# Two layers of chosen tokens get the row gather of a third, more weight pieces, and some operations tied to program order

## The chip, the cores and the metric

The kernel is one program on one core of one Trainium2 chip. Its time is the device time of one execution in microseconds. The core has engines that each take their instructions in order: PE (TensorE, matrix products), DVE (VectorE), ACT (ScalarE), POOL (GpSimd) and SP (SyncE, which here only issues transfers); ACT and POOL issue transfers too.

## The reference, cut to what matters

Two blocks run one after the other on 512 tokens of width 1024, everything in float32. The first mixes tokens and then sends each token to 2 of 64 experts. The second has two layers; each mixes tokens and then lets each of 16 experts choose 64 tokens:

```python
def expert_choice_ffn(h, router, w_gate, w_up, w_down):
    cap = EC_CAPACITY_FACTOR * n // N_EXPERTS_2          # 64
    aff = softmax(einsum('bnd,de->bne', h, router))
    gate, idx = lax.top_k(aff.transpose(0, 2, 1), cap)
    xg = h[bidx, idx]
    hid = silu(einsum('becd,edf->becf', xg, w_gate)) * einsum('becd,edf->becf', xg, w_up)
    y = einsum('becf,efd->becd', hid, w_down) * gate[..., None]
    return zeros_like(h).at[bidx, idx].add(y)
```

The input h of that function is a normalized and modulated x: `modulate(rms_norm(x, g), shift, scale)`, with shift and scale out of products of a conditioning vector with wide weights (w_mod in the first block, ada_w in the second). Each expert has 3 weight matrices of 2 MB.

## The kernel before, in words

Tokens lie as h, four tiles of 128 tokens by 1024. There are six stages in order: the first mixing stage, the 64-expert layer, the second mixing stage, the first expert-choice layer, the third mixing stage, the second expert-choice layer.

**Order.** Each stage is a set of generators that a planner (`weave`) steps by planned times; that gives the program order. The instructions then go to a scheduler that may put an instruction ahead of earlier ones on its engine when it takes its inputs to be there sooner. `keep_in_program_order(ins)` ties an instruction behind the one that precedes it on its engine in the program. Weights come by SP's transfers in the order of queues, into places that come free in turn (`pump`, L295).

**Products of a mixing stage** (`gemms`, L364) take fp32r parts: each weight piece is split into a high part by ACT (L386) and a low part, the rest, by DVE (L387), and each product is three. `split2` (L448, L449) does the same for single tiles. `rsqrt` (L168 to L173) is an inverse square root by some 14 small operations on DVE; its result scales a diagonal dg (L219) by which TensorE transposes and normalizes a tile. `mod_sum` (L2201 to L2207) multiplies rows of modulation weights by the conditioning vector and adds them up, on DVE and, where it shares, on POOL. In the first stage yd, a DRAM buffer of 4096 KB that the 64-expert layer scatters to, is filled by a POOL transfer (L686).

**The 64-expert layer** (`experts1`) works on pairs of experts. xd, a DRAM copy of the normalized rows, is written by the stage before it (`tail`, L2328). For each pair: P (L1262) is 1 where a token is in a place of an expert; four products (pid) give each place's row number; POOL gathers 128 rows xg of xd (L1250); eight TensorE transposes (pxt) turn them; ACT and DVE copy them with scale and shift into xT, 128 columns at a time (L1313, L1316). Pair 0 doesn't wait for xd: Pr = P times the normalizing factor (L1269), and 32 fp32 products of h with Pr give the same pxt.

**The expert-choice layers** (`ec`, L2591, with `experts`, L1089) find the 64th largest affinity by repeated top-8 on DVE, and from it the place of each token. x, the normalized rows, is split into fp32r parts xh and xl (`split_x`, `split_rest`), 32 KB a partition together. Four experts at a time, P (L1112) is built and 64 products pdis, 128 by 256, of xh and xl with P give xT, in two halves, by TensorE alone. Each pair then has 16 steps of gate and up products (pab), 4 transposes (phT), the down products (py), and products that add the results back to their tokens (pcm). Weights come as pieces of 512 KB in 24 places: 6, 9 and 9 in the first layer, 9 and 15 in the second.

```python
for part, x in enumerate((self.xh, self.xl)):
    self.mm(o, self.fcol(x[:, i], k), rhs, start=(i == 0 and part == 0), ...)
```

Of the kernel before, what the change touches and what calls it, by code (L numbers as in the profile page):

```python
# [137 lines left out]
class Kern:  # L138
# [23 lines left out]
    def rsqrt(self, pool, v, shape, tag):  # L162

        nc = self.nc
        ib = pool.tile(shape, I32, tag=tag + "i", name=tag + "i")
        y = pool.tile(shape, F32, tag=tag + "y", name=tag + "y")
        t = pool.tile(shape, F32, tag=tag + "t", name=tag + "t")
        nc.vector.tensor_scalar(ib, v.bitcast(I32), 1, None, op0=ALU.logical_shift_right)  # L168
        nc.vector.tensor_scalar(y.bitcast(I32), ib, -1.0, float(0x5F3759DF), op0=ALU.mult, op1=ALU.add)
        for _ in range(3):  # L170
            nc.vector.tensor_tensor(t, y, y, op=ALU.mult)
            nc.vector.scalar_tensor_tensor(t, t, -0.5, v, op0=ALU.mult, op1=ALU.mult)
            nc.vector.scalar_tensor_tensor(y, t, 1.5, y, op0=ALU.add, op1=ALU.mult)  # L173
        return y
# [189 lines left out]
    def gemms(self, items, pool, nb=2):  # L364
# [6 lines left out]
        def parts():  # L371
            for it in items:
                w, big = it["w"], None
                for c in it.get("order") or range(len(w.ev)):
# [11 lines left out]
                    nc.scalar.copy(hi, raw)  # L386
                    nc.vector.tensor_tensor(lo, raw, hi.bitcast(F32), op=ALU.subtract)  # L387
# [58 lines left out]
    def split2(self, hi, lo, x):  # L446

        self.nc.scalar.copy(hi, x)  # L448
        self.nc.vector.tensor_tensor(lo, x, hi.bitcast(F32), op=ALU.subtract)  # L449
# [34 lines left out]
    def run(self):  # L484
# [7 lines left out]
        self.nB, self.nX, self.nE = 14, 12, 24  # L492
# [65 lines left out]
    def mix1(self):  # L558
# [70 lines left out]
        def consts():  # L629
# [3 lines left out]
            yield 15000  # L633
            self.split2(wgh, wgl, wg)
# [17 lines left out]
        def start():  # L652
# [20 lines left out]
            for v, s in ((1, sx), (0, sl)):  # L673
# [6 lines left out]
                else:  # L680
# [5 lines left out]
            nc.gpsimd.dma_start(self.yd.rearrange("(p r) d -> p r d", p=128),  # L686
                                am.rearrange("p a b c t -> p (a b c t)").unsqueeze(1).to_broadcast([128, 2 * T // 128, D]))
# [300 lines left out]
        items = [item(wkc, sx, True, 2, k_in(sx), [sx.evx]), item(wvc, sx, False, 2, v_in(sx)),  # L988
# [25 lines left out]

    def split_x(self, pool):

        nc = self.nc
        for i in range(NT):
            if i < 3:
                t = pool.tile([128, D], F32, tag="xn", name="xn", bufs=2)  # L1020
                x = nc.scalar.activation(t, self.h[:, i, :], AF.Copy, scale=self.r[:, i:i + 1])
                if i == 0:
                    self.tc.keep_in_program_order(x)
                nc.scalar.copy(self.xh[:, i, :], t)
                for q in range(2):
                    c = slice(q * 512, (q + 1) * 512)
                    nc.gpsimd.tensor_tensor(self.xl[:, i, c], t[:, c], self.xh[:, i, c].bitcast(F32), op=ALU.subtract)
            else:
                nc.scalar.activation(self.xh[:, i, :], self.h[:, i, :], AF.Copy, scale=self.r[:, i:i + 1])

    def split_rest(self):
        for q in range(2):
            c = slice(q * 512, (q + 1) * 512)
            for i in range(3, NT):
                x = self.nc.vector.scalar_tensor_tensor(self.xl[:, i, c], self.h[:, i, c], self.r[:, i:i + 1], self.xh[:, i, c].bitcast(F32),
                                                        op0=ALU.mult, op1=ALU.subtract)
                self.tc.keep_in_program_order(x)

    def x_tiles(self, st, ne):
        xp = st.enter_context(self.pool("x", 1))  # L1040
        self.xh = xp.tile([128, NT, D], F32R, name="xh")
        self.xl = xp.tile([128, NT, D], F32R, name="xl")
        self.G = self.gates(ne)
        return xp
# [44 lines left out]
    def experts(self, ne, ws, pool, work, last=None):  # L1089


        nc = self.nc
        io = self.iota[:, 0:CAP]
        ng = ne // 4
        rX, rA, rY, rP = Res(2), Res(4), Res(3), Res(4)
        self.ny = 3
        evx, evy = [Ev() for _ in range(ng)], {(pr, c): Ev() for pr in range(ne // 2) for c in range(2)}
        xTs, PTs, gs, yos = {}, {}, {}, {}
        self.evf, evg = ([Ev() for _ in range(ne // 2)] for _ in range(2))

        evk = [Ev() for _ in range(KD // 2)]

        def dispatch(g):
            if g:
                yield evx[g - 1]
            yield rX
            yield rP
            yield rP
            es = slice(4 * g, 4 * g + 4)
            P = pool.tile([128, NT, 4, CAP], F32R, tag="P", name="P")  # L1110
            for i in range(NT):
                nc.vector.tensor_tensor(P[:, i], self.slot[:, i, es].unsqueeze(2).to_broadcast([128, 4, CAP]),  # L1112
                                        io.unsqueeze(1).to_broadcast([128, 4, CAP]), op=ALU.is_equal)
            if not g and ne == NE2:
                self.split_rest()
            xT = pool.tile([128, KD, 256], F32, tag="xT", name="xT", bufs=2)
            xTs[g] = xT
            yield 1500
            def transposed():
                for q in range(2):  # L1120
                    p = self.ps(name="ppt")
                    pp = lambda i: P[:, i, 2 * q:2 * q + 2, :].rearrange("p e s -> p (e s)").bitcast(F32)
                    for i in range(NT):
                        self.tr(p[:, i * 128:(i + 1) * 128], pp(i))
                    t = work.tile([128, T], F32R, tag="PT", name="PT", bufs=4)
                    nc.scalar.copy(t, p)
                    p = self.ps(name="pgt")
                    for i in range(NT):
                        self.mm(p[:, 0:2], pp(i), self.G[:, i, 4 * g + 2 * q:4 * g + 2 * q + 2], start=(i == 0), stop=(i == NT - 1))
                    gt = work.tile([128, 1], F32, tag="gt", name="gt", bufs=4)  # L1130
                    for j in range(2):
                        nc.vector.tensor_copy(gt[64 * j:64 * j + 64, :], p[64 * j:64 * j + 64, j:j + 1])
                    PTs[2 * g + q], gs[2 * g + q] = t, gt
                    self.fire(evg[2 * g + q], 800)
                    yield 0

            if g:
                yield from transposed()
            for k2 in range(KD // 2):
                p = self.ps(name="pdis")  # L1140
                for kk in range(2):
                    k = 2 * k2 + kk
                    o = p[:, kk * 256:(kk + 1) * 256]
                    for i in range(NT):
                        rhs = P[:, i].rearrange("p e s -> p (e s)")
                        for part, x in enumerate((self.xh, self.xl)):
# [13 lines left out]
        def ffn(pr):  # L1160
# [6 lines left out]
            for ws2 in up:  # L1167
                yield rA
                p = self.psum.tile([128, 512], F32, tag="a", name="pab", bufs=4)
                for k in range(KD):  # L1170
# [3 lines left out]
                    if k == 3:  # L1174
                        yield 0
# [1624 lines left out]
```

## Time and profile before

| | |
|---|---|
| runs of the kernel, us | 2719.69, 2713.5, 2715.77; median 2715.77 |
| profiled execution, us | 2713.79 |
| its span from the first to the last instruction, us | 2712.0 |
| mean granted TensorE clock (of full speed) | 0.957 |
| PE busy | 2353.7 us, 87% |
| DVE busy | 1121.4 us, 41% |
| ACT busy | 655.8 us, 24% |
| POOL busy | 261.2 us, 10% |
| moved by DMA | 772.76 MB, 285 GB/s on the mean |

Busy time is summed over stages with different limits, so it says little of the end; the profile's views by stretch, by wait and by time do. A wait is put down to what came last for it. In a timeline, the bracket is the idle time of the engine before the instruction and what ended it. The stages can be found by their time: the first mixing stage ends near 385 us, the 64-expert layer near 1503, the first expert-choice layer runs from about 1899 to 2182, the second from about 2418.

### The profile page before, as it was taken

How to read it: one execution, taken by the hardware profiler on the slowest of the kernel's cores; microseconds unless marked ns; L12 is line 12 of the kernel's file. 1: busy time of each engine (PE TensorE's matmuls, PEld its weight loads, DVE VectorE, ACT ScalarE, POOL GpSimd, SP SyncE). 2: the span in 40 equal slices, each digit the busy share in tenths (PEclk: the TensorE clock that was granted, in tenths of full speed). 3: DMA queues.
4: the chain of work that ended last, by engine and by line, in shares of the span. 5: the costliest groups of instructions: out<-in, count | busy, mean ns of one | idle time of the engine just before them, and what ended most of it. 6: DMA issues, size and time to landing. Idle time of an engine off the chain costs nothing. (4 is left out here: it accounts for less than half of the span.)

```text
span 2712.0 us, 32850 instructions
## 1 busy us (share of the span) xinstructions
PE 2353.7 (87%) x11807; PEld 1298.0 (48%) x11807; DVE 1121.4 (41%) x2915; ACT 655.8 (24%) x1357; POOL 261.2 (10%) x259
## 2 busy tenths in 40 slices
PE   1999998999989998888886587896999989979997
PEld 1677763334323432233322366685544368855442
DVE  2678653332342211111002679787222377452223
ACT  1642332232201101001000444343211032331111
POOL 0000011100110000000000312313000010110000
PEclk9999999999999999999998799997999999989999
DMA  8345559999999999999997434536899876249984
GB/s 310 108 133 156 195 216 357 348 349 376 351 395 396 344 409 408 406 405 402 407 407 299 137 90 142 164 120 231 318 381 352 310 240 215 71 168 383 407 319 173
DMA packets 270485, 772.76 MB, mean 285 GB/s; under 512 B 43103, under 2 KB 54511, under 8 KB 269808
## 3 DMA queue, kind: packets, MB, share of 16 engines
q1 hardware_dynamic: 255920, 744.72, 73.6%
q0 software_dynamic: 12960, 23.39, 2.5%
q10 hardware_dynamic: 1440, 2.52, 0.2%
q8 instruction: 94, 1.54, 0.2%
q14 instruction: 71, 0.58, 0.1%
HBM read 766.59 MB, written 27.79 MB: 293 GB/s over the span
## 5 line engine op out<-in xcount | busy, mean ns | idle before, releaser
L1421 PE MATMUL pab<-w,xT 128*64 128x512 f32 x3072 | 815.6, 602 | 21.9 <-DMA w<-in_w_dram 21.0
L1421 PEld LDWEIGHTS pab<-w,xT 128*64 128x64 f32 x3072 | 238.7, 136 | 480.4 <-issue 341.4
L1421 PE MATMUL py<-w,hT 128*64 128x512 f32 x1536 | 379.8, 630 | 39.3 <-ACT hT L1353 35.9
L1421 PEld LDWEIGHTS py<-w,hT 128*64 128x64 f32 x1536 | 116.8, 142 | 229.9 <-issue 166.1
L387 DVE TENSOR_TENSOR wl<-w,wh 128x512 fp32r<-128x512 f32 (+2 forms) x160 | 134.6, 850 | 98.7 <-ACT wh L386 94.9
L386 ACT CAST wh<-w 128x512 fp32r<-128x512 f32 (+2 forms) x160 | 109.4, 694 | 262.4 <-PE pg L466 178.2
L1345 DVE TENSOR_TENSOR hh<-hh,pab 128x512 f32<-128x512 f32 x32 | 22.0, 687 | 357.4 <-PE pab L1421 357.4
L1316 ACT ACTIVATE xT<-pxt,AB 128x128 f32<-128x128 f32 x190 | 70.2, 462 | 251.6 <-PE pab L1421 224.4
L1405 DVE TENSOR_TENSOR h<-h,pcm 128x512 f32<-128x512 f32 x144 | 91.9, 681 | 91.4 <-PE pcm L466 91.3
L1363 DVE TENSOR_TENSOR yf<-py,g 128x512 f32<-128x512 f32 x60 | 38.8, 685 | 214.5 <-PE py L1421 214.5
L466 PE MATMUL pg<-xh,wh 128*128 128x512 f32 x288 | 119.0, 416 | 9.2 <-DVE cv L1690 8.9
L1343 ACT ACTIVATE hh<-pab 128x512 f32<-128x512 f32 x32 | 19.1, 597 | 409.8 <-PE pab L1421 409.8
L466 PE MATMUL pg<-xl,wh 128*128 128x512 f32 x288 | 115.6, 401 | 0.0
L466 PE MATMUL pg<-xh,wl 128*128 128x512 f32 x288 | 115.4, 401 | 0.0
L2207 DVE SCALAR_TENSOR_TENSOR macc<-w,c,macc 128x512 f32<-128x512 f32 x116 | 90.0, 779 | 27.6 <-DMA w<-in_ada_w_dram 13.8
L1181 DVE TENSOR_TENSOR hh<-hh,pab 128x512 f32<-128x512 f32 x16 | 11.0, 687 | 185.4 <-PE pab L1421 185.4
L472 PE MATMUL phT<-CA,hh 128*128 128x128 f32 x192 | 32.2, 292 | 57.4 <-DVE hh L1345 46.9
L1250 POOL DMA_INDIRECT xg<-xd,nt x31 | 32.1, 1037 | 514.2 <-PE pxt L472 468.7
L466 PE MATMUL pdis<-P,xh 128*128 128x256 f32 x256 | 68.2, 303 | 4.6 <-DVE P L1112 4.6
L466 PE MATMUL pcm<-yh,PT 128*128 128x512 f32 x144 | 60.8, 437 | 8.7 <-ACT yh L1396 8.5
L466 PE MATMUL pdis<-P,xl 128*128 128x256 f32 x256 | 67.4, 300 | 0.0
L1396 ACT CAST yh<-yo 128x512 fp32r<-128x512 f32 x36 | 22.2, 618 | 185.3 <-DVE yo L1395 185.3
(758 smaller groups left out, 3716.6 us busy)
## 6 DMA issues: line engine op xcount, KB each, us to landing
w<-in_w_dram SPq DMA_DIRECT2D x768, 512.0 KB
w<-in_w_gate_dram SPq DMA_DIRECT2D x128, 512.0 KB
w<-in_w_up_dram SPq DMA_DIRECT2D x128, 512.0 KB
w<-in_w_down_dram SPq DMA_DIRECT2D x128, 512.0 KB
w<-in_ada_w_dram SPq DMA_DIRECT2D x164, 256.0 KB
w<-in_w_mod_dram SPq DMA_DIRECT2D x64, 256.0 KB
w<-in_sc_w_in_dram SPq DMA_DIRECT2D x24, 512.0 KB
w<-in_w_in_dram SPq DMA_DIRECT2D x40, 256.0 KB
```

The lines of the kernel that those rows point to most:

```text
L386: nc.scalar.copy(hi, raw)
L387: nc.vector.tensor_tensor(lo, raw, hi.bitcast(F32), op=ALU.subtract)
L466: ins = self.nc.tensor.matmul(out, lhsT, rhs, start=start, stop=stop)
L472: self.nc.tensor.transpose(out, in_, self.ident if ident is None else ident)
L1250: nc.gpsimd.indirect_dma_start(out=xg[pr % len(xg)], out_offset=None, in_=xd, in_offset=bass.IndirectOffsetOnAxis(ap=d, axis=0), bounds_ch ...
L1316: nc.scalar.activation(xT[:, k0 + k, :], p[:, k * 128:(k + 1) * 128], AF.Identity, scale=self.Af[:, k0 + k:k0 + k + 1], bias=self.Bf[:, k0 ...
L1345: nc.vector.tensor_tensor(hh, hh, ab[1], op=ALU.mult)
L1363: nc.vector.tensor_tensor(y[:, c * 512:(c + 1) * 512], ps[c], self.g2[:, c * 512:(c + 1) * 512], op=ALU.mult)
L1396: nc.scalar.copy(yh[:rows], y)
L1405: self.nc.vector.tensor_tensor(self.h[:, i, cs], self.h[:, i, cs], p, op=ALU.add)
L1421: self.nc.tensor.matmul(out, lhsT, rhs, start=start, stop=stop)
L2207: nc.vector.scalar_tensor_tensor(acc, w, s, acc, op0=ALU.mult, op1=ALU.add)
```

## The change

Five things are done together.

1. The expert-choice layers take the scheme of the 64-expert layer: `experts` and `experts1` become one function. xh and xl are gone. Pair 0 takes 32 products of h with Pr; pairs 1 to 7 have row numbers (`number`), a gather of xg on POOL into three buffers, eight transposes and copies of 128 columns. P is built for pairs 0 and 1 by themselves, then for four experts. The transposes of P for pair 0 (ppt, pgt) come after the second half of its products.
2. `tail` writes xd in the second and third mixing stage too: two ACT copies and two ACT transfers a tile, now behind the softmax of the tile, in buffers that another tensor has left.
3. The places for weight pieces are 30: 14, 9 and 7 in the first layer, 9 and 21 in the second.
4. These are tied to program order: the splits of the first items of products in the first and second mixing stage (wkc, wk), the split of the gate weights wg in the first (planned 2 us sooner), the first operation of the inverse square root "rf" that starts the second, the first operation of each modulation sum, and the fill of yd.
5. `final` (the last norm) takes two smaller tiles for its buffers.

```diff
+    def pin(self, ins):
+        self.tc.keep_in_program_order(ins)
...
-    def rsqrt(self, pool, v, shape, tag):
+    def rsqrt(self, pool, v, shape, tag, pin=False):
...
-        nc.vector.tensor_scalar(ib, v.bitcast(I32), 1, None, op0=ALU.logical_shift_right)
+        ins = nc.vector.tensor_scalar(ib, v.bitcast(I32), 1, None, op0=ALU.logical_shift_right)
+        if pin:
+            self.pin(ins)
...
-                    nc.scalar.copy(hi, raw)
-                    nc.vector.tensor_tensor(lo, raw, hi.bitcast(F32), op=ALU.subtract)
+                    both = [nc.scalar.copy(hi, raw), nc.vector.tensor_tensor(lo, raw, hi.bitcast(F32), op=ALU.subtract)]
+                    for ins in both if it.get("pin") else ():
+                        self.pin(ins)
...
-            yield 15000
-            self.split2(wgh, wgl, wg)
+            yield 13000
+            self.split2(wgh, wgl, wg, True)
...
-            nc.gpsimd.dma_start(self.yd.rearrange("(p r) d -> p r d", p=128),
-                                am.rearrange(...).unsqueeze(1).to_broadcast([128, 2 * T // 128, D]))
+            self.pin(nc.gpsimd.dma_start(self.yd.rearrange("(p r) d -> p r d", p=128),
+                                         am.rearrange(...).unsqueeze(1).to_broadcast([128, 2 * T // 128, D])))
...
-        items = [item(wkc, sx, True, 2, k_in(sx), [sx.evx]), ...
+        items = [dict(item(wkc, sx, True, 2, k_in(sx), [sx.evx]), pin=True), ...
...
-    def experts(self, ne, ws, pool, work, last=None):
+    def experts(self, ne, ws, pool, work, xd, xg, far=0, ids=None, tok=None, last=None):
...
-                yield ids[0]
-                gs[pr] = number(Pq, ids[1], 2 * pr, 2 * T, "id")
+                if ids:
+                    yield ids[0]
+                    gs[pr] = number(Pq, ids[1], 2 * pr, 2 * T, "id")
                 if pr:
...
+                    else:
+                        d = number(Pq, tok, 0, T, "id")
                     yield rG
                     fetch(pr, d)
                 if pr >= far:
+                    if not pr:
+                        yield evk[1]
                     yield rP
...
-                nc.gpsimd.tensor_tensor(o, w, s.to_broadcast([128, 512]), op=ALU.mult)
+                ins = nc.gpsimd.tensor_tensor(o, w, s.to_broadcast([128, 512]), op=ALU.mult)
...
+            if k == 0:
+                self.pin(ins)
...
+            for c in range(2):
+                x = xs(c)
+                nc.scalar.activation(x, self.h[:, i, c * 512:(c + 1) * 512], AF.Copy, scale=self.r[:, i:i + 1])
+                nc.scalar.dma_start(self.xd[i * 128:(i + 1) * 128, c * 512:(c + 1) * 512], x)
...
-            r = self.rsqrt(cp, s1, [128, NT], "rf")
+            r = self.rsqrt(cp, s1, [128, NT], "rf", True)
...
-        items = [dict(it, w=wk, ev={k: [hev[k]] for k in range(KD)}, cb=self.head_in(d, tp, 4, d.eyk)),
+        items = [dict(it, w=wk, pin=True, ev={k: [hev[k]] for k in range(KD)}, cb=self.head_in(d, tp, 4, d.eyk)),
...
-            parts = (9, self.nE - 9) if l else (6, 9, self.nE - 15)
+            parts = (9, 21) if l else (14, 9, 7)
...
-                self.split_x(rp)
...
-            self.weave(self.experts(E, ws, fp, fp, self.final(fp) if l else None))
+            xg = [fp.tile([128, D], F32, name=f"xg{j}") for j in range(3)]
+            self.weave(self.experts(E, ws, fp, fp, self.xd, xg, tok=tok, last=self.final(fp) if l else None))
```

## Rows read from the trace of the kernel before

**Rows 1.** page part 2: the span in 40 slices of 67.8 us, busy tenths
```profile
PE   1999998999989998888886587896999989979997
...
DMA  8345559999999999999997434536899876249984
```

**Rows 2.** waits of the first 140 us: engine, waited for, total, times, longest
```profile
PE pT L466 <- DVE dg L219: 52.9, 1, 52.9
...
ACT wh L386 <- DMA w<-in_w_in_dram: 36.9, 2, 35.8
...
DVE macc L2207 <- DMA w<-in_w_mod_dram: 6.6, 10, 1.5
```

**Rows 3.** timeline of VectorE, 0 to 90 us: start, us, operation [idle before]
```profile
12.09 0.17 DVE L168 TENSOR_SCALAR n1ci<-n1cv 128x2 int32<-128x2 int32 x1
48.10 0.43 DVE L387 TENSOR_TENSOR wl<-w,wh 128x256 fp32r<-128x256 f32 x1 [35.85 <-ACT wh L386]
...
84.53 0.24 DVE L672 SCALAR_TENSOR_TENSOR A<-A,V 128x8 f32<-128x8 f32 x2
```

**Rows 4.** timeline of SyncE's DMA queue, 0 to 90 us: start, us
```profile
32.34 4.84 SPq L321 DMA_DIRECT2D wbig<-in_w_mod_dram  x4
37.77 4.39 SPq L321 DMA_DIRECT2D w<-in_w_in_dram  x4
```

**Rows 5.** DMA issues of the first 90 us: KB each, us to landing
```profile
yd<-am POOLq DMA_DIRECT2D x1, 4096.0 KB, 24.7
```

**Rows 6.** a stretch of 5 us: busy PE, PEld, DVE, ACT, POOL, PEclk, DMA, GB/s
```profile
40.00:45.00 5.00, 0.00 (x0) 0.00 (x0) 0.00 (x0) 0.00 (x0) 0.00 (x0) 1.00 1.05 388
...
90.00:100.00 10.00, 7.16 (x48) 5.83 (x47) 10.00 (x22) 6.61 (x13) 1.36 (x2) 0.95 0.24 73
```

**Rows 7.** chain of waits, 1495 to 1550 us, in order of time
```profile
1505.22 9.15 DMA w<-in_ada_w_dram
...
1524.34 3.34 DMA w<-in_ada_w_dram
...
1530.32 2.65 DMA w<-in_ada_w_dram
```

**Rows 8.** timeline of VectorE, 1508 to 1530 us
```profile
1515.52 0.75 DVE L2207 SCALAR_TENSOR_TENSOR macc<-w,c,macc 128x512 f32<-128x512 f32 x1 [4.62 <-POOL macc L2201]
...
1519.02 0.69 DVE L387 TENSOR_TENSOR wl<-w,wh 128x512 fp32r<-128x512 f32 x1
...
1524.81 0.88 DVE L219 TENSOR_SCALAR dg<-CA,cfy 128x128 f32<-128x128 f32 x4
```

**Rows 9.** stretches of the first expert-choice layer, columns as in group 6
```profile
1900.00:1905.00 5.00, 5.00 (x31) 5.00 (x30) 1.68 (x4) 0.64 (x2) 0.00 (x0) 0.65 0.04 14
...
1930.00:1960.00 30.00, 29.11 (x168) 16.93 (x164) 8.41 (x19) 5.74 (x11) 0.00 (x0) 1.00 1.03 409
```

**Rows 10.** pdis alone, first and second expert-choice layer: us, PE, PEld, ACT
```profile
1899.00:2182.00 283.00, 36.16 (x256) 33.48 (x256) 16.35 (x32) 0.99 0.86 330
...
2418.00:2692.00 274.00, 37.48 (x256) 34.80 (x256) 16.34 (x32) 0.99 0.84 324
```

**Rows 11.** timeline of TensorE in the 64-expert layer, 384 to 400 us
```profile
386.39 4.01 PE L466 MATMUL pxt<-Pr,h 128*128 128x128 f32 x32
```

**Rows 12.** TensorE groups by form, 433 to 1450 us: busy, mean ns, idle before
```profile
L472 PE MATMUL pxt<-CA,xg 128*128 128x128 f32 x224 | 42.2, 309 | 0.0
...
L466 PE MATMUL pid<-rows,P 128*128 128x2 f32 x96 | 14.3, 253 | 10.6 <-DVE yf L1363 10.6
```

**Rows 13.** DMA issues, 433 to 1500 us
```profile
xg<-xd,nt POOLq DMA_INDIRECT x25, 6.8
```

**Rows 14.** timeline of VectorE, 1894 to 1906 us
```profile
1898.92 1.43 DVE L1112 TENSOR_TENSOR P<-slot,CA 128x256 fp32r<-128x256 f32 x4
```

**Rows 15.** VectorE groups by form, 330 to 400 us
```profile
L1262 DVE TENSOR_TENSOR P<-slot,CA 128x128 fp32r<-128x128 f32 x8 | 1.9, 281 | 0.0
...
L1269 DVE TENSOR_SCALAR Pr<-P,CA 128x128 f32<-128x128 f32 x4 | 0.9, 277 | 0.0
```

More of the change, by code (lines that the diff above doesn't have):

```diff
@@ L444, in gemms, with split2 @@
         return parts(), products()
-    def split2(self, hi, lo, x):
-        self.nc.scalar.copy(hi, x)
-        self.nc.vector.tensor_tensor(lo, x, hi.bitcast(F32), op=ALU.subtract)
+    def split2(self, hi, lo, x, pin=False):
+        both = [self.nc.scalar.copy(hi, x), self.nc.vector.tensor_tensor(lo, x, hi.bitcast(F32), op=ALU.subtract)]
+        for ins in both if pin else ():
+            self.pin(ins)
     def mod_split(self, tp, hi, lo, x, A, B, eng=None):
@@ L1013, in rank @@
         return v
[L1015 to L1044, printed above, removed]
     def gates(self, ne):
@@ L1265, in feed @@
                 if not pr:
-                    Pr = work.tile([128, NT, 128], F32, tag="PT", name="Pr", bufs=3)
+                    Pr = work.tile([128, NT, 128], F32, tag="PT", name="Pr", bufs=rT)
                     for i in range(NT):
@@ L1283, in feed @@
                         self.tr(p[:, i * 128:(i + 1) * 128], Pq(i).bitcast(F32))
[L1284 removed]
+                    t = work.tile([128, T], F32R, tag="PT", name="PT", bufs=rT)
                     nc.scalar.copy(t, p)
@@ L1378, in combine @@
                     self.combine(PTs[pr], yos[pr, c], i, c)
+                    if last and pr == np_ - 1:
+                        last(i, c)
                     yield 0
@@ L2468, in inv, with xs @@
             nc.gpsimd.dma_start(wr, a["router"][0].rearrange("(k p) f -> p k f", p=128))
-            for r, g in self.tail(tp, wr, NE2, evA2, evho, sp=cp):
+            rows = []
+            def xs(c):
+                if not rows:
+                    rows.append(bg.tile([128, 4, 512], F32, tag="zs", name="xs"))
+                rows.append(c)
+                return rows[0][:, len(rows) % 4]
+            for r, g in self.tail(tp, wr, NE2, evA2, evho, sp=cp, xs=xs):
                 self.spawn(r, g)
@@ L2716, in start, with xs @@
                 yield 0
-        ts = [bg.tile([128, T], F32, name=f"gx{m}") for m in range(4)]
+        ts = [bg.tile([128, T], F32, tag=f"gx{m}", name=f"gx{m}") for m in range(4)]
+        rows = []
+        def xs(c):
+            rows.append(c)
+            return bg.tile([128, 512], F32, tag=f"gx{len(rows) % 4}", name="xs")
         def c_in(half, j):
@@ L2752, in mix3 @@
         pa, pr = self.gemms(items, tp)
-        self.weave([(0, start()), (1, pa), (20, pr), (0, modt())] + self.tail(tp, wr, NE2, evA2, evho))
+        self.weave([(0, start()), (1, pa), (20, pr), (0, modt())] + self.tail(tp, wr, NE2, evA2, evho, xs=xs))
         st.close()
```

170 lines of the change are left out of this document (24 added, 146 removed).

## Prediction

> **What bounds the kernel now.** I read the page first. TensorE is nine tenths busy in most slices, but the first slice of 67.8 us stands at 1 and the slices around 1500 and 1850 us at 5 to 8 [rows 1]. So the kernel has TensorE-bound stretches (the two expert-choice layers), transfer-bound ones (the second half of the 64-expert layer, DMA 9), and three starts and ends of mixing stages where nobody is busy. The change touches a stretch of each kind, so each is priced by itself.
>
> Then the waits of the first 140 us. TensorE's first product waits 52.9 us for a diagonal built by VectorE, and ScalarE's first weight-piece copy waits 35.8 us for its DMA [rows 2]. The timeline of VectorE says how these hang together: it is in the middle of the first inverse square root (n1ci at 12.09), then does nothing for 35.85 us until the low part of a weight piece, which needs ScalarE's copy [rows 3]. The norm's next step, with all its inputs ready, stands behind that subtract on the engine, and the squares of h stand behind the copy on ScalarE. The work of the stage is therefore held by the order, and the transfer that it is held by is late because 512 KB pieces of whh to wbig and a 4096 KB fill of yd are ahead of it [rows 4, 5] at a full rate of 388 GB/s [rows 6].
>
> The chain of waits at the start of the second mixing stage shows the same in small: ada_w pieces of 9.15, 3.34 and 2.65 us [rows 7], and on VectorE a multiply-add (4.62 us of idle before it) and weight splits in between the steps of a square root whose result, dg, comes at 1524.81 [rows 8]. In the expert-choice layers a 30 us stretch has 29.11 us of TensorE at full clock with DMA at 1.03 [rows 9]: there only less TensorE work helps.
>
> **First start, part by part.** The pins take the three wkc splits, the wg split and the first multiply of each modulation sum out of the place in front of the norm; the yd fill goes behind POOL's earlier work, out of the queue of the first 48 us. The 36 us of norms, transposes, row products and A (48.10 to 84.53 [rows 3]) then begin where VectorE stopped, at 12.3, and A is due at 84.53 - 35.85 = 48.7. It is held by transfers only if these come later: without yd, 4.19 MB / 388 GB/s = 10.8 us, the w_in piece that landed at 47.7 lands at 36.9, and wbig, issued ahead of it [rows 4], lands before that. Both are under 48.7, so the whole 35.85 is gained. What is late next: VectorE also waits 6.6 us in that stretch for w_mod pieces [rows 2], which come after w_in. If these multiply-adds fall behind A, the start gains up to 42; but some 18 of them at 0.75 us (the duration of one in [rows 8]), 13 us, then stand in a stretch in which VectorE is already full (10.00 of 10 from 90 to 100 us [rows 6]), which leaves 23. If only yd leaves the path, 10.8. yd's own 4 MB then shares the queues later, where slice 2 has DMA at 3 tenths [rows 1]; I cost it at nothing since its first user is hundreds of us away; without that cover it is 10.8. I take **-35**, bounds -11 and -42.
>
> **Second and third mixing starts.** Between the ready sum and dg, VectorE spends 4.62 us idle for POOL's ada_w piece, and then three multiply-adds at 0.75 and three splits at 0.69 that are no part of the square root [rows 8]: 4.6 + 2.3 + 2.1 = 9 us. The pinned first step and the pinned splits put these behind dg. Against it, the ada_w sums start later, and they come back on the chain as 3.34 and 2.65 us [rows 7]. I take **-8**, bounds -15 (both waits go too) and +6 (the root gains nothing and both are paid again). The third start has one pinned multiply, about -1.
>
> **Expert-choice layers, each.** Removed: 256 products pdis, which keep TensorE busy 36.16 and 37.48 us a layer [rows 10]. Added: pair 0 by 32 fp32 products of h with P*r. The same operation took 4.01 us in the 64-expert layer [rows 11]; the layer begins at a granted clock of 0.65 (part of it at 1.2 GHz, the rest at 2.4) after an idle TensorE [rows 9], which doubles the first half of them: some 6 us. Pairs 1 to 7: eight transposes each, 42.2 us for 224, so 1.51 a pair, and four products that give the row numbers, 14.3 for 96, so 0.60, with 10.6 us of waits in 24 pairs, 0.44 [rows 12]: 2.55 x 7 = 17.9. Before the first product there are four P of 128x128 and four Pr, 0.95 + 0.9 us [rows 15], where a first P of four was enough (1.43 / 4 = 0.36 [rows 14]): +1.5. Sum: -36.2 + 6 + 17.9 + 1.5 = -10.8, and -12.1 in the second layer. The rest is hidden: the removed hi/lo split of x ran on ScalarE and POOL beside the top-64 search; the eight row copies and DMA issues a layer sit on ScalarE, which is idle most of the tail, only the last tile's (1 to 2 us) can show; the gather lands 6.8 us after its issue [rows 13] and is asked for a pair ahead, of about 34 us (274 / 8 [rows 10]); uncovered, it would cost that on each of 7 pairs. Six more weight pieces let 3.1 MB more come early, worth nothing while TensorE is the bound: 8 x 12.6 MB and 3.7 MB of gathers less 15.7 MB prefetched make 89 MB, 218 us at 409 GB/s [rows 9], under the 262 that stay of 274. Bounds a layer: -18 (TensorE's waits for P go too, and the clock rises as early as now), and +4 (a wait of 2 us more each pair for numbers or transposes' copies). Two layers: **-22**, bounds -36 and +8.
>
> On the price of fp32: the row has 125 ns for an fp32 product of 128 columns, about what a pdis record of 256 columns takes (36.16 / 256 = 141 ns, the slow start included) [rows 10, 11], so twice per column. The Trainium skill ("FP8 and Floating Point Precision", TensorE Precision Notes) counts four passes for true fp32, which speaks against trading fp32r for fp32. By it, estimated from four times the pdis price, 32 products take 32 x 4 x 71 = 9.0 us, and the two layers gain 10 us less. The row is of the very operation, so the sum goes by it and the rule gets no chance of its own.
>
> **Sum.** -35 - 8 - 1 - 22 = -66 on the profiled execution's 2713.8: 2648. The median of the runs stands 2 us above it, so **2650 us**.
>
> **Rivals.** (1) The first start is only half undone: the splits leave, but the multiply-adds stay between the norm's steps or fall into VectorE's full stretch, or only yd's bytes count. For it: VectorE full after 90 us [rows 6]. Against: the 12 us after n1ci wait for nothing but order [rows 3]. -11 to -23 in place of -35: 2662 to 2674, say 2668. (2) The expert layers gain nothing, since every pair now passes TensorE, VectorE, TensorE, POOL, DMA, TensorE, and number products wait behind yf [rows 12]: 2672. (3) The other side: gathers late. A pair's numbers are pinned to no place; if they are computed when the pair before ends, TensorE waits 6.8 us for landing [rows 13] and 1 to 3 us for the steps before, on 7 pairs and 2 layers: 14 x 7.8 to 9.8 = +109 to +137 on the 2650, about 2770. It decides against the change from 66 / 14 = 4.7 us a pair on. Against it: the 64-expert layer does the same, and its transposes show no idle time before them [rows 12]; but there transfers set the pace. (4) The pins do nothing or displace other work as large: 2715.
>
> **How the numbers follow.** Runs differ by some 0.2% (5.4 us), the limit of what can be told from no change. Forecast (2650 within 15) 0.50; rival 1 alone 0.17; rival 2 alone or with it 0.20; more than forecast (starts -42 and -15, layers -36: down to 2622) 0.06; rival 3 0.04; rival 4 0.03. Rival 3 is slower and 4 within 0.2%; so slower 0.04, within 0.03, faster 0.93. The range from 2625 to 2690 leaves out the ends of both sides, some 2 in 10.
>
> **What would show it.** Right: TensorE's first product near 15 us, A near 49, w_in's first copy near 37; dg of the second stage 9 us earlier after its sum; in the layers 32 pxt and 56 transposes in place of 36 us of pdis, no wait of pxt for xg, TensorE still 29 of 30. Wrong: VectorE or ScalarE waiting for w_in or w_mod before 40 us; pxt waiting on DMA; a TensorE share under 28 of 30 between pairs; the second mixing stage ending no earlier after its start than now.

## The result, and the profile after

The changed kernel takes 2685.08 us (median; 2682.72 to 2687.34), the kernel before on the same chip 2716.32: a ratio of 0.9884, 95% interval 0.9867 to 0.9902, so 31 us less. The prediction was 2650, within 2625 to 2690. The time lies in the range, which was wide; the gain is 31 of the 66 us that were forecast. The profiled execution of the changed kernel took 2683.5 us (2713.8 before).

Where it came from can be read by the times at which the same work begins and ends in the two traces. pg are the products of a mixing stage with its weights; pxt, pcm and the others are as in the kernel's description; prank and pngt (in the views below) are the counts that open a layer and give each token its place. "Moved by" is what the stretch itself gained (-) or lost (+); the first row is a part of the second, and the six rows from the second on add up to -31:

| stretch, us | before | changed | moved by | forecast |
|---|---|---|---|---|
| first product pg of the first stage | 86.1 | 45.8 | -40.3 | -36 |
| first stage, to the first pxt | 386.4 | 359.5 | -26.9 | -35 |
| 64-expert layer, to its last pcm | 1501.5 | 1478.4 | +3.8 | 0 |
| second stage, to prank of the first layer | 1896.7 | 1865.9 | -7.7 | -8 |
| first expert-choice layer, to its last pcm | 2182.6 | 2156.6 | +4.8 | -10.8 |
| third stage, to prank of the second layer | 2416.0 | 2389.6 | -0.4 | -1 |
| second expert-choice layer, to its last pcm | 2698.4 | 2667.4 | -4.6 | -12.1 |

The two starts came about as forecast; the first stage gave a third of its gain back on the way, and the layers gave nothing between them. The page's slices of TensorE and of the queues, against [rows 1], show the first start filled (6 in place of 1), and the slices of the first expert-choice layer no fuller than before:

```profile
PE   6999998999989988888886678896999989979997
...
DMA  7544589999999999999996444436989876269993
```

The waits of the first 100 us after, against [rows 2]: the first product waits for its diagonal 14.3 us and not 52.9; the waits for w_in have got smaller, not gone: there are four of them now, of up to 4.0 us.

```profile
PE pT L474 <- DVE dg L225: 14.3, 1, 14.3
...
ACT wh L392 <- DMA w<-in_w_in_dram: 10.9, 4, 4.0
...
DVE macc L2064 <- DMA w<-in_w_mod_dram: 7.0, 6, 4.6
```

The timeline of VectorE after, against [rows 3]: n1ci's next steps follow at once, dg comes at 13.94, the splits stand behind the norms, and A is there at 44.26 in place of 84.53.

```profile
11.77 0.17 DVE L172 TENSOR_SCALAR n1ci<-n1cv 128x2 int32<-128x2 int32 x1
11.97 0.17 DVE L175 TENSOR_SCALAR n1cy<-n1ci 128x2 int32<-128x2 int32 x1
...
13.94 0.48 DVE L225 TENSOR_SCALAR dg<-CA,n1cy 128x128 f32<-128x128 f32 x2
...
43.06 1.10 DVE L392 TENSOR_TENSOR wl<-w,wh 128x256 fp32r<-128x256 f32 x3 [2.90 <-ACT wh L392]
...
44.26 0.24 DVE L680 SCALAR_TENSOR_TENSOR A<-A,V 128x8 f32<-128x8 f32 x2
```

A part of what took back a third is in the next views: POOL's timeline has the fill of yd at 61.89, 16 us behind the first pg, and the stretches of 5 us (columns as in group 6) have the queues full behind it. Before, as far behind the first pg, a stretch of 15 us has 202 GB/s (the third view). The pieces of w_in that the products need are in the same queues, and the four waits of 10.9 us fall between 61 and 76 us; with the fill put off, 2.5 us of them are left (below).

```profile
60.27 1.67 POOL L466 TENSOR_TENSOR hl<-ms,hh 128x512 fp32r<-128x512 f32 x1
61.89 0.86 POOL L694 DMA_DIRECT2D yd<-am  x1
```

```profile
55.00:60.00 5.00, 2.04 (x9) 1.31 (x9) 5.00 (x11) 1.49 (x5) 0.38 (x1) 1.00 0.00 0
...
65.00:70.00 5.00, 5.00 (x34) 4.30 (x33) 1.94 (x4) 0.99 (x3) 0.00 (x0) 1.00 1.03 417
70.00:75.00 5.00, 1.86 (x11) 1.26 (x9) 2.45 (x4) 0.80 (x2) 0.00 (x0) 1.00 1.04 418
```

```profile
100.00:115.00 15.00, 15.00 (x55) 10.35 (x56) 9.61 (x16) 11.23 (x18) 3.58 (x3) 0.89 0.70 202
```

The start of the second stage after, against [rows 8]: VectorE goes from the sum to dg without a foreign instruction, in 4.5 us (1487.68 to 1492.13; 1510.72 to 1524.81 before).

```profile
1487.68 0.17 DVE L2297 TENSOR_SCALAR s<-s 128x4 f32<-128x4 f32 x1 [0.85 <-ACT junk L202]
...
1489.96 0.17 DVE L172 TENSOR_SCALAR cfi<-vf 128x4 int32<-128x4 int32 x1
...
1492.13 0.88 DVE L225 TENSOR_SCALAR dg<-CA,cfy 128x128 f32<-128x128 f32 x4
```

The first expert-choice layer after: TensorE's timeline (start, us) at its start, and the stretches of 5 us there.

```profile
1869.30 9.96 PE L474 MATMUL pxt<-Pr,h 128*128 128x128 f32 x64 [2.88 <-DVE Pr L1118]
1879.19 1.94 PE L1278 MATMUL pab<-w,xT 128*64 128x512 f32 x8
1881.06 0.65 PE L480 MATMUL ppt<-CA,P 128*128 128x128 f32 x4
1881.56 0.95 PE L474 MATMUL pgt<-CA,P 128*128 128x2 f32 x8
1882.37 0.59 PE L474 MATMUL pid<-tokf,P 128*128 128x2 f32 x4
...
1883.31 0.95 PE L474 MATMUL pgt<-CA,P 128*128 128x2 f32 x8
1884.19 1.77 PE L1278 MATMUL pab<-w,xT 128*64 128x512 f32 x2
```

```profile
1875.00:1880.00 5.00, 5.00 (x41) 4.42 (x41) 1.03 (x3) 1.37 (x3) 0.00 (x0) 1.00 1.02 409
1880.00:1885.00 5.00, 5.00 (x36) 3.45 (x32) 1.90 (x10) 1.63 (x3) 0.81 (x1) 0.94 1.02 409
1885.00:1890.00 5.00, 5.00 (x17) 2.49 (x15) 1.08 (x4) 0.00 (x0) 0.30 (x1) 0.50 1.03 411
1890.00:1895.00 5.00, 5.00 (x20) 3.37 (x20) 0.93 (x6) 0.58 (x1) 2.03 (x2) 0.50 1.02 396
1895.00:1900.00 5.00, 5.00 (x17) 2.29 (x16) 1.74 (x6) 1.87 (x2) 0.00 (x0) 0.50 0.77 224
```

Pair 0 is 64 records and 9.96 us, not 32 and 4.01 [rows 11]. After it and eight records of pab comes a row of small work: transposes (ppt), and products of two columns (pgt, pid). Behind that row the granted clock goes from 1.00 to 0.50, its lower level of 1.2 GHz, and stays there for some 20 us, though TensorE is busy all the time; the two pab at 1884.19 take 1.77 us together (the same two take 1.07 at full clock in the second layer). In the layers of before the clock stays at 1.00 after its rise [rows 9], but for a dip of some 4 us in the second.

### The profile page after: what moved, and what is told of

Its sections match the earlier page's. It is cut to its first block, busy times and chain, and to the rows that moved or that the text cites. A ratio compares the mean times of both kernels' runs of the same rounds, so it can differ in the third digit from the quotient of the medians.

```text
span 2681.4 us, 32578 instructions
## 1 busy us (share of the span) xinstructions
PE 2353.6 (88%) x11591; PEld 1277.6 (48%) x11591; DVE 1137.4 (42%) x2993; ACT 651.3 (24%) x1387; POOL 257.0 (10%) x261
## 5 line engine op out<-in xcount | busy, mean ns | idle before, releaser
L1278 PE MATMUL pab<-w,xT 128*64 128x512 f32 x3072 | 833.4, 607 | 22.6 <-DMA w<-in_w_dram 21.7
L1278 PE MATMUL py<-w,hT 128*64 128x512 f32 x1536 | 383.8, 631 | 40.3 <-ACT hT L1208 40.3
L1171 ACT ACTIVATE xT<-pxt,AB 128x128 f32<-128x128 f32 x282 | 104.6, 461 | 395.8 <-PE pab L1278 232.3
L1198 ACT ACTIVATE hh<-pab 128x512 f32<-128x512 f32 x48 | 28.7, 597 | 531.9 <-PE pab L1278 531.8
L1168 DVE TENSOR_SCALAR xT<-pxt,AB 128x128 f32<-128x128 f32 x102 | 41.6, 409 | 96.6 <-ACT xT L1171 96.3
L480 PEld LDWEIGHTS pxt<-CA,xg 128*128 128x128 f32 x360 | 49.4, 208 | 55.7 <-issue 46.5
L474 PE MATMUL pcm<-yh,PT 128*128 128x512 f32 x144 | 64.0, 453 | 11.4 <-ACT yh L1253 10.6
L1252 DVE SCALAR_TENSOR_TENSOR yo<-py,gt,g 128x512 f32<-128x512 f32 x36 | 27.0, 749 | 102.6 <-PE py L1278 101.3
L474 PEld LDWEIGHTS pg<-xh,wh 128*128 128x128 f32 x288 | 55.1, 191 | 28.0 <-issue 10.6
```

The source lines that it names most:

```text
L474: ins = self.nc.tensor.matmul(out, lhsT, rhs, start=start, stop=stop)
L480: self.nc.tensor.transpose(out, in_, self.ident if ident is None else ident)
L1168: nc.vector.tensor_scalar(xT[:, k0 + k, :], p[:, k * 128:(k + 1) * 128], self.Af[:, k0 + k:k0 + k + 1], self.Bf[:, k0 + k:k0 + k + 1], op0 ...
L1171: nc.scalar.activation(xT[:, k0 + k, :], p[:, k * 128:(k + 1) * 128], AF.Identity, scale=self.Af[:, k0 + k:k0 + k + 1], bias=self.Bf[:, k0 ...
L1198: nc.scalar.activation(hh, p, AF.Silu)
L1278: self.nc.tensor.matmul(out, lhsT, rhs, start=start, stop=stop)
```

## The experiments

Each is the changed kernel or the kernel before with one edit. All were compared with the kernel before on their own chip, whose median was 2721 to 2722 us there, so ratios and times of stretches are compared, not medians of different chips. "Layer" below is the time from a layer's first prank to its last pcm, read from the timeline of TensorE: 285.9 and 282.4 us before, 290.7 and 277.8 in the changed kernel.

**The ties alone.** The kernel before with all the ties of part 4 of the change, and with the expert-choice layers, the tail and the 24 places of before.

> The kernel before with all the ties to program order and nothing of the expert-choice layers, the pieces or xd. Theory: the ties alone bring what the change gained outside the two expert-choice layers, so the first products 386 to 359 us (27), the 64-expert layer gives 4 back, the second start gains 8: 2682 to 2690, at most 5 us from the changed kernel. Rival (the layers carry a good part of the gain): over 2695.

0.9882 (0.9864 to 0.9901): the whole of the gain. The first pxt comes at 361.2 (386.4 before), the second stage's first transposes 14.1 us after the last pcm (23.7 before).

**The layers alone.** The changed kernel without the added ties, and the split of wg planned as before:

```diff
     def pin(self, ins):
-        self.tc.keep_in_program_order(ins)
+        pass
```

> The changed kernel with every added tie to program order taken away (wg planned at 15000 again). Theory: the first layer loses 4.8 us and the second gains 4.5 in the changed kernel, so the new scheme is worth nothing: 2710 to 2722. Rival, by the prediction's sum: -22, 2694.

1.0021 (1.0004 to 1.0038): nothing gained, perhaps 6 us lost. The layers took 287.3 and 277.9 us, 1.4 more and 4.5 less than before; the first stage ended 5.0 us later than before, which the layers don't explain.

**Which ties.** One kind of tie is taken away at a time:

```diff
-                    for ins in both if it.get("pin") else ():
+                    for ins in ():
...
-        for ins in both if pin else ():
+        for ins in ():
```

> The changed kernel without the ties of the splits (wkc, wg, wk). Theory: the low parts stand in front of the first norm on VectorE again and wait for w_in, which lands about 42 us after the start since yd's fill is behind it; A at 74 to 79 and the first product pg at 76 to 80 (45.8 in the changed kernel, 86.1 before); of these 30 us later, 15 to 25 are left at the end, since the fill then falls in a stretch that waits for nothing: -6 to -16 against the kernel before. Rival (yd's fill or the sums freed the start): A under 50 still.

0.9983 (0.9959 to 1.0006). As expected, VectorE stands behind the low part again, for 25.54 us now that yd's fill is behind w_in, and A comes at 69.03, 5 us sooner than expected:

```profile
11.98 0.17 DVE L172 TENSOR_SCALAR n1ci<-n1cv 128x2 int32<-128x2 int32 x1
37.69 0.42 DVE L392 TENSOR_TENSOR wl<-w,wh 128x256 fp32r<-128x256 f32 x1 [25.54 <-ACT wh L392]
...
39.39 0.43 DVE L455 TENSOR_TENSOR wbgl<-wbg,wbgh 128x256 fp32r<-128x256 f32 x1 [0.40 <-ACT wbgh L455]
...
69.03 0.24 DVE L680 SCALAR_TENSOR_TENSOR A<-A,V 128x8 f32<-128x8 f32 x2
```

But I had expected 15 to 25 us of loss at the end, and the loss was all of the stage's gain: the first pxt came at 387.5, though pg began 15.5 us sooner than before. Where the lead went can be placed: at the gate product plg it is still 15.8 us (88.3 against 104.1), at the first pmod, which ends a modulation sum, 3.5 (122.3 against 125.8). In between the fill of yd keeps the queues full, in this stretch of 15 us:

```profile
85.00:100.00 15.00, 9.97 (x38) 5.86 (x36) 8.06 (x14) 8.25 (x12) 2.19 (x2) 0.90 0.98 358
```

The granted clock is 0.73 to 0.93 besides, from 70 to 145 us, in such stretches (0.89 to 1.00 before). What each of the two takes was not tried.

```diff
-            if k == 0:
-                self.pin(ins)
```

> The changed kernel without the tie of each modulation sum's first operation. Theory: the first multiply by w_mod stands inside the first norm again and waits for its piece, issued at 35.4: dg at 39 to 42, A at 68 to 74, so the splits' ties alone bring some 12 of the 40 us; and the start of the second mixing stage loses its 9.6 us: -5 to -16 against the kernel before. Rival (the splits alone held the norms up): A under 50 and -25 or better.

1.0005 (0.9988 to 1.0022). The multiply waits for its piece in the middle of the first norm, and the second stage's first transposes come 21.6 us after the last pcm again:

```profile
39.95 0.49 DVE L2062 TENSOR_SCALAR macc<-w,cm 128x512 f32<-128x512 f32 x1 [26.68 <-DMA w<-in_w_mod_dram]
...
41.87 0.48 DVE L225 TENSOR_SCALAR dg<-CA,n1cy 128x128 f32<-128x128 f32 x2
...
75.45 0.24 DVE L680 SCALAR_TENSOR_TENSOR A<-A,V 128x8 f32<-128x8 f32 x2
...
97.14 0.42 DVE L455 TENSOR_TENSOR wbgl<-wbg,wbgh 128x256 fp32r<-128x256 f32 x1
```

Nothing was left of the 5 to 16 us that were expected. So both the splits' ties and the sums' ties were needed; either, left out, brings the stall back. The sums' tie is also the one that brought most of the second start; without the splits' ties that start stayed at 15.5 us (14.0 in the changed kernel). The tie of the inverse square root "rf" was not taken away by itself.

**The fill of yd**, later:

```diff
-            self.pin(nc.gpsimd.dma_start(self.yd..., am...))
...
             self.fire(evR, 1000)
+            yield 3000
+            self.pin(nc.gpsimd.dma_start(self.yd..., am...))
```

> The changed kernel, with the fill of yd issued some 35 us later, behind the last constants, where the queues moved 2 to 12 GB/s. Theory: the fill in the stream of w_in pieces (10.9 us of waits for them) is what took back most of the first start's 40 us; without it 7 to 11 us come back: 2674 to 2678. Rival: VectorE's multiply-adds, or TensorE being the bound, took it back: 2682 to 2687, the waits gone but the stage's end where it was.

0.9873 (0.9857 to 0.9890), not told apart from the changed kernel's 0.9884. The stage by itself did what was expected. prank of the 64-expert layer ended at 347.6, and at 350.2 and 349.1 in the two more runs with the late fill below; in the changed kernel it ended at 353.1, in five more runs with the fill in its place at 353.9 to 358.8. The means are some 6 us apart: that is what the fill costs this stage.

The waits for w_in have gone to 2.5 us in all, and yet pg to plg still took 26.4 us (18.0 before). VectorE's multiply-adds, five of which now fall between the two, are not the reason: in the run without the sums' ties none does, and it takes 28.5. It goes with the splits' ties: all runs that have them take 25.8 to 29.2 us from pg to plg, the three without them (before, the layers alone, the splits untied) 16.8 to 18.0. plg needs, through the small products pzg, the split of the gate weights wg (wbgh, wbgl), and its tied place is 20 us behind the first pg, where it was 31 to 36 us ahead of it; here it comes at 65.06, the first pg at 44.4.

```profile
65.06 0.42 DVE L455 TENSOR_TENSOR wbgl<-wbg,wbgh 128x256 fp32r<-128x256 f32 x1
```

Whether plg's delay is carried to the stage's end is not shown: the run without the splits' ties has plg early and loses its lead behind it.

The end did not show the 6 us: in the profiled execution, the slowest of the four, the clock fell in both layers (290.6 and 287.6).

The fill, left in its old place:

```diff
-            self.pin(nc.gpsimd.dma_start(self.yd..., am...))
+            (nc.gpsimd.dma_start(self.yd..., am...))
```

> The changed kernel with the fill of yd alone left untied, so that it is issued at 4.5 us again. Theory: the splits' ties are what frees the first start; the w_in pieces land at 48 in place of 42.6 and the first product pg comes at 49 to 51 in place of 45.8, but the pieces after them are not held up, so the stage ends 0 to 6 us sooner than in the changed kernel: -31 to -37 against the kernel before. Rival (the fill's place is what freed the start): A near 55 or later and +5 to +10 on the changed kernel.

0.9908 (0.9890 to 0.9925), -25 us where -31 to -37 was expected. The start was as expected but for 3 us (A at 52.09, pg at 53.6). The stage did not end sooner: the first pxt comes at 363.8, against 359.5 in the changed kernel and 360.3 to 365.2 in five more runs with its first stage. So the splits' and sums' ties free the start without the fill's, and the fill's place, worth some 8 us at pg, is not seen at the stage's end.

All the ties and the late fill, with the layers of before:

> The ties alone, with the layers of before, and the fill of yd issued behind the last constants as in the run with the late fill. There the first stage ended 5.5 us sooner. Theory: -31 - 5 = -36 against the kernel before. Rival (the first stage's end is not carried on to the end): -31.

0.9873 (0.9851 to 0.9895), 2686.35 against 2721.54: -35, close to the theory's -36, though its interval holds the rival's -31 too.

**The clock in the layers.** First the changed kernel again:

> The changed kernel itself once more, beside the others on their chip: -31 against the kernel before, and the clock falls to half for about 20 us after the start of the first expert-choice layer, in the second perhaps.

0.9886 (0.9866 to 0.9906), the same; but now the clock held in the first layer and fell in the second, 282.5 and 287.3 us. The stretches of the two at the same distance from the start:

```profile
1885.00:1890.00 5.00, 5.00 (x38) 3.46 (x34) 1.90 (x9) 1.63 (x3) 0.62 (x1) 1.00 1.03 411
1890.00:1895.00 5.00, 5.00 (x32) 2.96 (x31) 2.21 (x10) 0.58 (x1) 1.52 (x2) 1.00 1.02 407
...
2403.00:2408.00 5.00, 5.00 (x37) 3.59 (x34) 1.65 (x8) 1.87 (x4) 0.35 (x1) 0.99 0.45 151
2408.00:2413.00 5.00, 5.00 (x16) 2.33 (x14) 1.54 (x5) 0.00 (x0) 0.70 (x1) 0.50 0.53 175
2413.00:2418.00 5.00, 5.00 (x19) 3.05 (x18) 0.93 (x6) 0.59 (x1) 2.02 (x2) 0.50 0.55 160
```

The same instructions in the same order, once with and once without a fall: 290.7 against 282.5 in the first layer, 287.3 against 277.8 in the second. Eight of the traces leave the row of small products as it is (the changed kernel is two of them), and the clock fell in 12 of their 16 layers. A fall has one of two lengths: added up over the first 80 us, the stretches lack 3.4 to 3.8 us of full clock without a fall (the rise alone), 9.5 to 9.7 with a short one and 14.1 to 14.8 with a long one. Seven of the eight have 30 places, and their layers are in the order of these lengths:

| clock in the layer | first layer, us | second layer, us |
|---|---|---|
| no fall | 282.5 | 277.8, 277.9 |
| short fall, about 6 us of clock | 287.3, 287.7, 287.9 | 283.3, 283.4 |
| long fall, about 11 us of clock | 290.4, 290.6, 290.7 | 287.3, 287.6, 289.2 |

So a fall costs 5 to 11 us, about what it takes of the clock, and whether it comes isn't settled by the program.

Then with the row spread out:

```diff
             for pr in range(np_):
+                if not far and pr > 1:
+                    yield self.evf[pr - 1]
                 g, q = pr // 2, pr % 2
```

> The changed kernel, with the numbers, the gather and the transposes of P for pairs 2 to 7 of the expert-choice layers held back until the pair before starts its products. Theory: the row of small products in the first 25 us of a layer is what TensorE's clock fell after (0.50 for 20 us in the first layer) and what costs switches between products; spread out, the clock stays at 1.00 and the first layer gains 8 to 10 us, the second 0 to 3: 2672 to 2678. Rival: the clock falls all the same, because the first such row stays: 2681 to 2687. If gathers come late by it, pxt waits for xg and the time rises.

0.9869 (0.9853 to 0.9886), not told apart from the changed kernel. The first layer took 279.5 us, with a dip of 3 us left; the second 285.7, for another reason: a gather came late, TensorE waited 7.6 us for it, and the clock fell within that wait.

Then with ppt and pgt of a pair as a task of their own, the numbers and gathers one to two pairs ahead, and a second buffer for P:

```diff
+                if pr and not far:
+                    yield evk[1] if pr < 3 else self.evf[pr - 2]
...
+        def turn():
+            for pr in range(np_):
+                yield evp[pr]
+                yield self.evf[pr - 1] if pr else evk[1]
+                if pr < 2:
+                    yield 4000
+                Pq = Ps[pr]
...
-            parts = (9, 21) if l else (14, 9, 7)
+            parts = (9, 20) if l else (14, 9, 6)
```

> The changed kernel, but in the expert-choice layers the transposes of P and the gates (ppt, pgt) of each pair are a task of their own that waits for the products of the pair before, and the numbers and gathers run one to two pairs ahead; P has two buffers for it and the pieces are 29. Theory: with the small products spread and no gather late, the clock stays at 1.00 and both layers take some 278 us from prank to the end (290.7 and 277.8 in the changed kernel): 11 us less than the changed kernel, -42 against the kernel before. Rival (the clock falls for another reason): within 4 us of the changed kernel, -31.

0.9876 (0.9854 to 0.9897). In the first layer all came true: clock at 1.00, 278.2 us. In the second a gather was late again, and the clock fell to 0.50 about 1 us into that wait, for some 13 us: 286.5. TensorE's timeline there:

```profile
2441.10 0.61 PE L474 MATMUL pid<-tokf,P 128*128 128x2 f32 x4
...
2442.88 0.63 PE L480 MATMUL phT<-CA,hh 128*128 128x128 f32 x4
2450.89 1.95 PE L480 MATMUL pxt<-CA,xg 128*128 128x128 f32 x8 [7.38 <-DMA xg<-xd,id]
...
2454.26 15.79 PE L1310 MATMUL pab<-w,xT 128*64 128x512 f32 x64
```

The pair's numbers (pid, 2441.10) stand three short groups (ppt, pgt, phT) ahead of its transposes (2450.89), and the gather between them takes its 7 us [rows 13] with nothing else on TensorE.

The same, with numbers as early as the buffers allow, and the late fill of above (the lines against the run just told):

```diff
-                if pr and not far:
-                    yield evk[1] if pr < 3 else self.evf[pr - 2]
+                if pr == 1 and not far:
+                    yield evk[1]
```

> The changed kernel with the fill of yd behind the last constants, and ppt and pgt of each pair held back as in the run before, but the numbers and gathers as early as the three buffers allow (there one gather came 7.4 us late in the second layer and the clock fell to half for 18 us after it). Theory: clock at 1.00 and no wait for xg in both layers, some 278 us each from prank to the end, and the first stage ends 4 to 6 us sooner: -31 - 12 - 5, so -44 to -50 against the kernel before. Rival (the layers' clock falls for a reason other than rows of small products): -33 to -38.

0.9878 (0.9857 to 0.9899), no better. The clock held at both starts, as it did at all six starts with the row spread, but for the dip of 3 us, and no transposes waited for xg; yet the layers took 286.3 and 284.0 us. So neither theory holds: the clock did not fall again, and a clock that holds is not enough. Against the unfallen layers of the table (282.5 and 277.8) spreading the row gained 3 to 4 us in the first layer of two runs (279.5, 278.2), and here it lost 4 and 6. In this first layer the queues moved 408 or 409 GB/s from 1987 to 2107 (first view), but in the run before, with 278.2 us, they did so from 1960 to 2110 (second view), so full queues alone don't tell the two apart. Charged from start to start, pab takes 142.6 us here and 138.5 there; what holds it up is not shown.

```profile
1987.00:2017.00 30.00, 28.83 (x124) 12.89 (x120) 12.36 (x23) 5.09 (x11) 0.00 (x0) 1.00 1.03 409
...
2077.00:2107.00 30.00, 27.66 (x108) 9.80 (x104) 8.62 (x13) 2.32 (x4) 0.00 (x0) 1.00 1.03 408
```

```profile
1990.00:2020.00 30.00, 29.66 (x128) 13.69 (x128) 14.25 (x26) 5.08 (x11) 0.00 (x0) 1.00 1.03 409
...
2080.00:2110.00 30.00, 28.47 (x115) 10.14 (x113) 7.18 (x12) 1.80 (x3) 0.00 (x0) 1.00 1.03 409
```

**The places for pieces.**

```diff
-            parts = (9, 21) if l else (14, 9, 7)
+            parts = (9, 15) if l else (6, 9, 9)
```

> The changed kernel with the places of before: 6, 9 and 9, and 9 and 15. Theory: TensorE is the bound in the layers, so six places do nothing: within 3 us of the changed kernel, -28 to -34 against the kernel before. Rival: the fewer pieces lie ready at a layer's start, the sooner the gathers and weights together (409 GB/s for most of the first layer) hold TensorE up: +5 or more, with pab waiting for DMA.

0.9907 (0.9886 to 0.9929), and the layers 295.5 and 284.3 us. The first had a short fall, the second none; against the table's rows of 30 places that is 8 and 6.5 us more. In the first 30 us of the first layer the queues moved 298 GB/s, against 404 in the run without the splits' ties, which has 30 places and a short fall too; charged from start to start, pab and py took 8.2 us longer than there. So both layers speak for the rival, and the six places are worth some 7 us a layer in this execution. It is the slowest of its four, though: by the ratios its median is some 6 us above the changed kernel's in all, and the intervals of the whole times meet.

## Why the prediction was wrong, point by point

- **The first start, -35: the mechanism right, a cover missing.** Order held the norms, and the ties freed them: A at 44.3 (48.7 forecast, with the multiply-adds behind it, as in the bound of 42). The step that failed here is "yd's own 4 MB then shares the queues later, [...] I cost it at nothing". Its price without cover was given as 10.8; the late fill shows some 6 of the 13 us that the stage gave back. The rest is gone by plg already (pg to plg takes 8.4 us longer than before with the late fill), where the tied split of wg comes late; the sum put that tie at nothing too, and what it costs at the end is not shown. Rival 1 is not what happened: the multiply-adds did move behind A, but in the run that has none of them there pg to plg took as long.
- **The second and third starts, -8 and -1:** 7.7 and 0.4. The size was right, the ties that were named for it only in part: the pinned splits are worth 1.5 of the 9.7 us between pcm and the transposes, the sums' ties 7.6.
- **The 64-expert layer, left out of the sum:** it took 3.8 us longer in the changed kernel. That it is bound by transfers in its second half [rows 1], so that an earlier start is not carried through whole, is not shown to be the reason: in all thirteen other traces it takes 1.2 to 4.7 us longer than in that of the kernel before, the two that start it later among them.
- **The layers, -22, is the step that failed**: the sum put at nothing what the instructions that stay would lose, and it had no term for a fall of the clock. Rival 2's number came true for the layers, and not by its reason. Charging TensorE's time to the instruction that started last, for the second layer, where the clock held in both traces (but for the dip of 4 us before):

| us of TensorE, start to next start | before | changed | difference | forecast |
|---|---|---|---|---|
| pdis | 36.4 | 0 | -36.4 | -37.5 |
| pair 0 (pxt of Pr) | 0 | 9.2 | +9.2 | +6 |
| pairs 1 to 7 (pxt of xg) | 0 | 7.9 | +7.9 | +10.6 |
| pid | 0 | 3.2 | +3.2 | +7.3 with waits |
| start (pngt to the first product) | 2.6 | 3.1 | +0.6 | +1.5 |
| pcm | 37.3 | 42.0 | +4.7 | 0 |
| pab | 132.1 | 135.2 | +3.0 | 0 |
| pgt, ppt, phT, py | 73.7 | 76.9 | +3.2 | 0 |

The removed and added work comes to -15.5, better than the sum's -12.1, though the pair 0 row was misread: the 32 records of [rows 11] are one half of that pair's products, the other half came later in that layer. What the sum lacked is the 11 us that the old instructions take longer. In the first layer, where the clock held in the second trace of the changed kernel, it is the same: -13.8 for the work and +10.3 for the old instructions. The waits are a small part (pcm waits 3.0 us for yh, 2.3 before). TensorE changes from one kind of product to another 161 times in place of 121; what a change costs was not tried, so the cause of the 11 us is argued only.

```profile
L474 PE MATMUL pcm<-yh,PT 128*128 128x512 f32 x64 | 28.9, 458 | 3.4 <-ACT yh L1253 3.0 <-DVE xT L1168 0.4
...
L474 PE MATMUL pxt<-Pr,h 128*128 128x128 f32 x64 | 9.3, 317 | 2.9 <-DVE Pr L1118 2.9
L480 PE MATMUL pxt<-CA,xg 128*128 128x128 f32 x56 | 8.7, 296 | 0.0
```

Then the clock: the forecast doubled the first half of pair 0 for the slow start and had no term for a later fall. The clock falls again in most of the layers, and that takes 5 to 11 us each time: the first layer, 285.9 us before, takes 282.5 where the clock holds and 290.7 in the trace of the changed kernel. That the two layers come to nothing together, +4.8 and -4.6, is the chance of that execution: with no fall they would be some 8 us better, with two long ones 10 to 12 us worse.
- **"Worth nothing while TensorE is the bound"**, of the six pieces, was wrong by the one trace there is: 218 us of transfers in 262 is an average, and the places hold 1.25 pairs. With six fewer the layers take 6.5 to 8 us more, and the queues move less at the first layer's start (298 GB/s and not 404).
- **The fp32 price.** The 4.0 us of [rows 11] were for half of pair 0's products; a fp32 product is two records here, and pair 0 has 64 records, 9.2 to 10.0 us with the slow start. A product is 2 x 125 ns, against 71 for the same 128 columns of a pdis record, 3.5 times as much. The Trainium skill ("FP8 and Floating Point Precision", TensorE Precision Notes) counts four passes for true fp32. The trace agrees with it within what the slow start leaves open: the prediction's estimate by it was 9.0 us.
- **Rival 3**, the late gather, did not come in the changed kernel (1.4 us in the first layer) but in two of the experiments, at 7.4 and 7.6 us, with a fall of the clock within the wait.

What stays open: whether the late split of wg costs anything at the first stage's end; how the fill and the clock share the 12 us lost when only the splits were untied; why the old instructions of the layers take 11 us longer; why the clock falls in one execution and not in another; why spread work with an early start of the numbers took longer at full clock; and what would make the layers faster than some 278 us, now that TensorE and the queues are both near full.

## What to carry to other kernels

When a scheduler may move instructions, look in the timeline of each engine for work that waits for nothing and stands behind an instruction that waits for a transfer; here the ties alone brought all 31 us, and with the splits or the sums left untied almost nothing was gained. A tie also holds its instruction back: look at what needs it next. A transfer that is put off must be put into a stretch whose queues are idle in the new timeline, not in the old one. Where small products replace large ones, count the whole set of records of the model row, and add what the neighbours lose; and look at the granted clock behind them before calling the trade a gain.

## What the runs showed of the hardware

TensorE's clock fell to 0.50 (1.2 GHz) while TensorE was busy for 5.00 of 5 us, behind 3 us of 128-column transposes and two-column products, and came back some 20 us later during 512-column products; the same program did it in the one layer in one execution and in the other in the next. The falls came in two lengths, which took about 6 and 11 us of clock and 5 to 11 us of the layer's time. In waits of 7.4 and 7.6 us for a gather it fell to 0.50 as well. A fp32 product of 128 columns is two records of 125 ns each; a record of the fp32r product pdis, with 256 columns, took 141 ns, slow start included.
